# A hybrid decoder layer on one core: the residual written out in two halves, an accumulator fetched in five parts, and the last token tile in block order

## The chip, the core and the metric

The kernel runs on one core of one Trainium2 chip. The metric is the time of one execution on the device in microseconds (us). Three timed runs of the kernel before gave 2352.08, 2352.68 and 2355.79 us; their median, 2352.68 us, is the time before. One more execution was recorded with a profile.

The engines are named as the profile names them: PE is the matrix engine (PEld its weight loads), DVE the vector engine, ACT the scalar engine, POOL the general engine, and SP the engine that issues most of the DMA transfers. A "q" behind the name (SPq) means the sequencer of that engine. SP's transfers run on queue 1 (hardware_dynamic) and POOL's on queue 0 (software_dynamic) of the same 16 DMA engines.

## The reference

One layer over 512 tokens, with 16 learned meta tokens ahead of them (528 rows), model width 2048, feed-forward width 5632, all in float32. The first half of the layer is a mixer of two groups of heads (a gated short convolution and a linear recurrence with decay) and an output projection. What the change touches comes after it:

```python
mix = jnp.concatenate([y_conv, y_rwkv], axis=-1) @ w_out
h = h + rmsnorm(mix, g_post_mix)                       # the residual
f = conv_glu(rmsnorm(h, g_pre_ffn), w_gate_up, conv_ffn, w_down)
h = h + rmsnorm(f, g_post_ffn)
return h[:, N_META:]

def conv_glu(x, w_gate_up, conv_ffn, w_down):
    gu = x @ w_gate_up
    gate, up = jnp.split(gu, 2, axis=-1)
    gate = causal_dwconv(gate, conv_ffn)               # three taps along the tokens
    return (jax.nn.silu(gate) * up) @ w_down
```

The residual h is thus needed twice: normalized, as the input of the feed-forward part, and at the very end, when the normalized result of that part is added to it.

## The kernel before, in words

**Data.** In the first half the activations lie transposed: the model dimension on 128 partitions in 16 tiles h(0) to h(15), the tokens along the free dimension. Matmuls are done in a reduced float32 form, each operand split into a high and a low part ("hi", "lo"; H and O for weights), and the product taken as three matmuls.

**The feed-forward part** has 5632 = 44 tiles of 128 features (f = 0 to 43), in 11 groups of four. A step `seven(f)` makes gate and up of one f in seven products of half matrices, after a Strassen scheme; each product is a *unit* of the main loop. When a group's four f are done, its products with `w_down` are added to an accumulator: `down7` with 14 units for groups 1 to 9, `down` with eight units for the first group (four blocks of 512 columns by two parts), and `last_part` for the last group. The first units that concern the change are units 7 to 14 of the main loop, those of the first down group.

**The accumulator.** Its rows of tokens 256 to 511 stay on the chip in the tile `acc`. Those of tokens 0 to 255 are added in DRAM (`accd`), and so is one of the Strassen products that is kept aside (`acce`). Near the end `reload` brings both back: accd in three fetches on SP into the tiles `hb` and `hs`, and acce in two transfers on POOL that add onto `acc`, all at one place, three units behind the first unit of f = 41.

**One memory, two lives.** The tiles that later are `hb`, `hs` and `acc` first hold the residual: h(0) to h(5) in hb, h(6) and h(7) in hs, h(8) to h(15) in acc. The residual must be out of them before the new contents come: acc is first written behind unit 8, hs in the last part of f = 4's own chain (unit 10) and hb in that of f = 6.

**Turning the residual** (`turned`): the residual must be written to `out` with tokens as rows, so that the tail can fetch it again. In 16 steps (four m-tiles by 128 tokens each) DVE turns four blocks with STREAM_TRANSPOSE into a buffer, hxh and hxl in turn, and SP writes the buffer out in four transfers. These two buffers are also used, afterwards, for the high and low part of hidden activations. The steps are taken in the loops of f = 2 and f = 3, and what is left is run after them.

**The order of work.** A class `Plan` records operations and lays them out by rank (a lower rank goes first) and estimated cost; `plan.step(3)` gives its operations rank 3, the ordinary rank is 2, and matmuls that may fill gaps have the rank `FILL` (9). The mixer, f = 0 to 3 and the tail are laid out so. In the main loop the order of PE, DVE, ACT and POOL is that of the code, unit after unit: the matmuls of unit k, what follows unit k-1, the events of unit k, and the preparation of unit k+2. `at(k, fn)` adds an event to unit k. The order of SP in the main loop isn't the code's: a scheduler sets it. Each engine works through its instructions in order.

**The tail** (`last_part`, `finish`): the token tiles are done as (2, 3), then 0, then 1. For each tile and each block n of 512 columns, twelve matmuls (four f by three products) end a sum in PSUM, DVE adds it to the accumulator, ACT squares and sums the row, and the block is multiplied by the norm's weights gp. When all four blocks are in, the row's scale is computed by small operations (`rb`), and `finish` scales the row, adds the residual, fetched from `out` into a tile of the name tt, and writes the result.

Of the kernel before, what the change touches and what calls it, by code (L numbers as in the profile page):

```python
# [10 lines left out]
F32 = mybir.dt.float32  # L11
F32R = mybir.dt.float32r
AF = mybir.ActivationFunctionType
ALU = mybir.AluOpType
# [73 lines left out]

HEAD3 = 4.0

# [421 lines left out]
def hymba(tc, I, out, ysp=None):  # L512
# [59 lines left out]
    def run(g):  # L572
        for _ in g:
            pass
# [684 lines left out]
    with ExitStack() as ctx2:  # L1259
# [377 lines left out]

        def turned():


            for m in range(0, KT, 4):
                for i in range(0, SEQ, 128):
                    t = p2.tile([128, 2 * HW], F32, name=("hxh", "hxl")[i // 128 % 2], bufs=1)[:, :512]
                    v = t.rearrange("p (j m c) -> p j m c", j=4, m=4)
                    for k in range(4):
                        V.transpose(v[:, :, k], h(m + k)[:, 2 + i:130 + i].rearrange("p (j c) -> p j c", j=4))
                    for q in range(4):
                        c = 512 * q + 32 * m
                        SP.dma_start(out[i:i + 128, c:c + 128].rearrange("(j b) c -> b j c", j=4),
                                     t[32 * q:32 * q + 32].rearrange("p (j c) -> p j c", j=4))  # L1650
                    yield
# [53 lines left out]
        su = sums(T2, T3)  # L1705
        tr = turned()
# [24 lines left out]
        run(su)  # L1731
        with plan.step(3):
            run(tr)

# [45 lines left out]
        def seven(f):  # L1780
# [62 lines left out]
            if f < NF - 1:  # L1843
# [135 lines left out]

        def reload():  # L1980
            acc01.extend([p2.tile([128, 3072], F32, name="hb", bufs=1), p2.tile([128, 2, 512], F32, name="hs", bufs=1)])
            SP.dma_start(acc01[0][:, :2048], accd[1])
            SP.dma_start(acc01[0][:, 2048:], accd[0, :, :1024])
            SP.dma_start(acc01[1].rearrange("p n c -> p (n c)"), accd[0, :, 1024:])
            for t in range(2):
# [71 lines left out]
        m2 = st[:, :4]  # L2057
        r3 = {}

        def last_part(i):  # L2060
# [4 lines left out]

            def down_some(t, n, o, ii):
                for f in ii:
                    with plan.step(2, FILL):
                        down_pe(NG - 1, t, o, lambda f: last_w(2 * n + f // 2), (f,))

            early = {(n, t): bank(t) for n in range(0 if i else 2) for t in ts}
            for n, t in early:
                down_some(t, n, early[n, t], range(GF - 1))
            for n in range(D // 512):
                for t in ts:
                    o = early.get((n, t)) or bank(n if len(ts) == 1 else t)
                    down_some(t, n, o, range(GF - 1 if (n, t) in early else 0, GF))
                    with plan.step(0 if n == 3 else 2):
                        add_up(NG - 1, t, n, o)
                        if i == 0 and n == 1 and t == ts[0]:  # L2080
# [3 lines left out]
                        x = total(t, n)  # L2084
                        S.activation(out=junk[:, 2 * n + t % 2], in_=x, func=AF.Square,
                                     accum_out=st[:, 4 + 4 * t + n:5 + 4 * t + n])
                    with plan.step(3):
                        (G if i == 0 and n < 3 else V).tensor_tensor(out=x, in0=x, in1=gp[:, 512 * n:512 * n + 512], op=ALU.mult)
            for t in ts:
                a = st[:, 20 + 8 * t:28 + 8 * t]  # L2090
                ss, m, r, q, o = (a[:, k:k + 1] for k in range(5))
                with plan.step(0):
                    V.tensor_reduce(out=ss, in_=st[:, 4 + 4 * t:8 + 4 * t], axis=AX.X, op=ALU.add)
                    V.scalar_tensor_tensor(out=m, in0=ss, scalar=1.0 / D, in1=m2[:, t:t + 1], op0=ALU.mult, op1=ALU.add)
                    rsqrt_guess(m, r, q)
                    S.activation(out=r, in_=r, func=AF.Copy, scale=-0.5)
                    V.scalar_tensor_tensor(out=o, in0=q, scalar=-3.0, in1=r, op0=ALU.add, op1=ALU.mult)
                r3[t] = o

        def finish(t):  # L2100
            to = out[128 * t:128 * t + 128]
            if t != LAST[-1][0]:
# [3 lines left out]
                return  # L2106
            x = total(t, 3)
            S.activation(out=x, in_=x, func=AF.Copy, scale=r3[t])
            G.tensor_tensor(out=x, in0=x, in1=hh[:, 1536:], op=ALU.add)
            for n in range(3):  # L2110
                x = total(t, n)
                V.scalar_tensor_tensor(out=x, in0=x, scalar=r3[t], in1=hh[:, 512 * n:512 * n + 512], op0=ALU.mult,
                                       op1=ALU.add)
                SP.dma_start(to[:, 512 * n:512 * n + 512], x)
            SP.dma_start(to[:, 1536:], total(t, 3))

# [98 lines left out]
```

## Time and profile before

| what | value |
|---|---|
| median of the three timed runs | 2352.68 us (2352.08 to 2355.79) |
| the profiled execution | 2357.65 us |
| its span, first to last instruction | 2355.7 us |
| its mean granted PE clock | 0.993 of full speed |
| PE busy | 2307.1 us, 98% of the span |
| DVE, ACT, POOL busy | 1847.3, 1357.1, 661.4 us |
| bytes moved by DMA | 347.58 MB, mean 148 GB/s |

A row of a timeline or of the chain of waits begins with the start in us from the span's first instruction, then the length in us, then engine, source line, operation, out<-in by the program's names, shapes and "xN" for N instructions in one row; brackets at the end tell how long the engine stood idle before and what released it. All instructions of the recorded parts have the line of the recording helper, L231, so they are told apart by tile. Rows of a window give its length and the busy time and number of instructions of PE, PEld, DVE, ACT and POOL, then the granted PE clock, the busy share of the DMA engines and GB/s.

### The profile page before, as it was taken

How to read it: one execution, taken by the hardware profiler on the slowest of the kernel's cores; microseconds unless marked ns; L12 is line 12 of the kernel's file. 1: busy time of each engine (PE TensorE's matmuls, PEld its weight loads, DVE VectorE, ACT ScalarE, POOL GpSimd, SP SyncE). 2: the span in 40 equal slices, each digit the busy share in tenths (PEclk: the TensorE clock that was granted, in tenths of full speed). 3: DMA queues.
4: the chain of work that ended last, by engine and by line, in shares of the span. 5: the costliest groups of instructions: out<-in, count | busy, mean ns of one | idle time of the engine just before them, and what ended most of it. 6: DMA issues, size and time to landing. Idle time of an engine off the chain costs nothing.

```text
span 2355.7 us, 46510 instructions
## 1 busy us (share of the span) xinstructions
PE 2307.1 (98%) x18032; PEld 2180.4 (93%) x18032; DVE 1847.3 (78%) x2612; ACT 1357.1 (58%) x2653; POOL 661.4 (28%) x887
## 2 busy tenths in 40 slices
PE   9999999999999999997999999999999999999998
PEld 8999999999999999996998989898989898989896
DVE  7687898878754677785598879797978888888776
ACT  7666766767654556663455555555555555555545
POOL 0131746455351012510012131313131313131312
PEclk9999999999999999998999999999999999999999
DMA  5544333333433755745448494858584848585765
GB/s 183 156 132 118 88 96 89 103 103 107 127 105 90 226 174 162 157 112 131 124 121 210 126 215 126 207 133 206 131 208 118 212 128 200 131 193 139 189 182 139
DMA packets 169954, 347.58 MB, mean 148 GB/s; under 512 B 35682, under 2 KB 56548, under 8 KB 169092
## 3 DMA queue, kind: packets, MB, share of 16 engines
q1 hardware_dynamic: 135492, 269.07, 36.7%
q0 software_dynamic: 34240, 75.53, 19.3%
q8 instruction: 142, 2.33, 0.4%
q14 instruction: 80, 0.66, 0.1%
HBM read 279.11 MB, written 65.42 MB: 146 GB/s over the span
## 4 chain that ended last, share of the span: by engine, by line
PE 85%; DVE 5%; DMA 4%; issue 2%; ACT 2%; POOL 1%; SPq 1%; DVEq 0%; ACTq 0%; POOLq 0%
PE mps L231 56%; PE u L231 14%; PE d L231 8%; PE st L231 4%; PE aux L231 2%; DVE O L231 2%; ACT H L231 1%; DVE raw L231 1%; SPq L231 1%; DMA R<-w_gu_dram 1%; DMA R<-w_down_dram 0%; DVE acc L231 0%; DMA l<-lo 0%; DMA hs<-xT_dram 0%; DMA hb<-xT_dram 0%
## 5 line engine op out<-in xcount | busy, mean ns | idle before, releaser
L231 DVE TENSOR_TENSOR O<-R,H 128x1024 fp32r<-128x1024 f32 x455 | 598.3, 1315 | 171.4 <-ACT H L231 152.4
L231 ACT CAST H<-R 128x1024 fp32r<-128x1024 f32 x455 | 470.2, 1049 | 158.8 <-PE u L231 60.4
L231 PE MATMUL mps<-ahi,whi 128*128 128x264 f32 (+2 forms) x1792 | 359.9, 289 | 6.1 <-ACT ahi L231 5.6
L231 PE MATMUL mps<-alo,whi 128*128 128x264 f32 (+2 forms) x1792 | 360.5, 289 | 0.3 <-DVE alo L231 0.2
L231 PE MATMUL mps<-ahi,wlo 128*128 128x264 f32 (+2 forms) x1792 | 358.4, 288 | 1.2 <-DVE wlo L231 1.0
L231 POOL TENSOR_TENSOR raw<-raw,rb 128x514 f32<-128x514 f32 (+2 forms) x45 | 93.6, 2080 | 736.7 <-DVE raw L231 503.7
L231 PE MATMUL mps<-tt,H 128*128 128x258 f32 (+1 forms) x2160 | 288.6, 284 | 5.3 <-ACT H L231 4.5
L231 PEld LDWEIGHTS mps<-ahi,whi 128*128 128x128 f32 x1792 | 273.8, 189 | 8.9 <-ACT ahi L231 5.6
L231 DVE TENSOR_TENSOR wlo<-raw,whi 128x512 fp32r<-128x512 f32 (+1 forms) x261 | 193.8, 748 | 109.8 <-ACT whi L231 90.6
L231 PEld LDWEIGHTS mps<-tt,H 128*128 128x128 f32 x2160 | 273.3, 190 | 6.8 <-ACT H L231 4.7
L231 PEld LDWEIGHTS mps<-ahi,wlo 128*128 128x128 f32 x1792 | 273.8, 189 | 3.8 <-DVE wlo L231 1.6
L231 PE MATMUL mps<-ahi,H 128*128 128x258 f32 (+1 forms) x1064 | 259.3, 284 | 18.4 <-DVE raw L231 16.4
L231 PEld LDWEIGHTS mps<-alo,whi 128*128 128x128 f32 x1792 | 273.8, 189 | 3.4 <-DVE alo L231 1.2
L231 PE MATMUL mps<-alo,H 128*128 128x258 f32 (+1 forms) x1064 | 259.3, 283 | 0.5 <-DVE alo L231 0.5
L231 ACT CAST whi<-raw 128x512 fp32r<-128x512 f32 (+1 forms) x261 | 156.7, 604 | 162.9 <-PE mps L231 87.3
L231 DVE TENSOR_TENSOR R<-R 128x1024 f32<-128x1024 f32 x190 | 232.6, 1224 | 5.2 <-DMA R<-w_down_dram 1.4
L231 PEld LDWEIGHTS mps<-ahi,H 128*128 128x128 f32 x1064 | 199.8, 191 | 19.0 <-ACT H L231 16.5
L231 PEld LDWEIGHTS mps<-alo,H 128*128 128x128 f32 x1064 | 199.7, 191 | 0.7 <-DVE alo L231 0.7
L231 POOL TENSOR_SCALAR SUV<-VT 32x64 f32<-32x64 f32 x272 | 129.2, 475 | 161.4 <-PE st L231 136.9
L231 PE MATMUL mps<-ahi,O 128*128 128x258 f32 (+1 forms) x1064 | 158.2, 284 | 0.0
L231 PE MATMUL mps<-tt,O 128*128 128x258 f32 (+1 forms) x1080 | 153.6, 282 | 0.0
L231 PEld LDWEIGHTS mps<-ahi,O 128*128 128x128 f32 x1064 | 141.4, 191 | 0.0
(396 smaller groups left out, 4490.3 us busy)
## 6 DMA issues: line engine op xcount, KB each, us to landing
R<-w_gu_dram SPq DMA_DIRECT2D x176, 512.0 KB, 5.6
raw<-w_in_dram SPq DMA_DIRECT2D x208, 256.0 KB, 2.7
R<-w_down_dram SPq DMA_DIRECT2D x88, 512.0 KB, 4.6
R<-w_gu_dram POOLq DMA_DIRECT2D x40, 512.0 KB, 6.2
accd<-raw POOLq DMA_DIRECT2D x54, 256.0 KB, 6.6
accd<-q POOLq DMA_DIRECT2D x54, 256.0 KB, 7.4
R<-w_down_dram POOLq DMA_DIRECT2D x18, 512.0 KB, 7.8
raw<-w_out_dram SPq DMA_DIRECT2D x32, 256.0 KB, 3.9
```

Source lines behind the costliest of these rows:

```text
L231: return getattr(self.real, op)(*real, **{k: x.get() if isinstance(x, View) else x for k, x in kw.items()})
```

## The change

It has three parts.

1. `turned` becomes one step with the buffer as its argument. The eight steps of the acc half (m = 8 and 12) are taken in the loop of f = 3, at the ordinary rank. The eight steps of the half in hb and hs (m = 4, then 0) become `aside(i)`, two per unit in units 10 to 13, into buffers of the names raw and q. The last part of f = 4's chain, which overwrites hs, moves three units later.
2. `reload` gets an argument, and its five transfers are placed 8, 10, 12, 14 and 16 units behind the first unit of f = 41.
3. In `last_part` the twelve matmuls of a block of tiles 0 and 1 become one step with a rank of its own, so that blocks come in order; the sum of the first three columns of squares is taken and scaled with block 2, the row's scale takes one ACT step less on the way (gp is scaled by -0.5 beforehand), and the multiplies by gp are POOL's for tiles 2 and 3, all eight, and DVE's for the others. `finish` of the last tile has three multiply-adds of 768, 768 and 512 columns on DVE with one transfer each, in place of three of 512 on DVE with a fourth block on ACT and POOL.

```diff
-HEAD3 = 4.0
+HEAD3, ENDS = 4.0, ((0, 768), (768, 1536), (1536, 2048))
...
-        def turned():
-            for m in range(0, KT, 4):
+        def turned(t, m, i):
+            v = t.rearrange("p (j m c) -> p j m c", j=4, m=4)
+            for k in range(4):
+                V.transpose(v[:, :, k], h(m + k)[:, 2 + i:130 + i].rearrange("p (j c) -> p j c", j=4))
+            for q in range(4):
+                c = 512 * q + 32 * m
+                SP.dma_start(out[i:i + 128, c:c + 128].rearrange("(j b) c -> b j c", j=4),
+                             t[32 * q:32 * q + 32].rearrange("p (j c) -> p j c", j=4))
+
+        def turns():
+            for m in (8, 12):
                 for i in range(0, SEQ, 128):
-                    t = p2.tile([128, 2 * HW], F32, name=("hxh", "hxl")[i // 128 % 2], bufs=1)[:, :512]
...
+                    turned(p2.tile([128, 2 * HW], F32, name=("hxh", "hxl")[i // 128 % 2], bufs=1)[:, :512], m, i)
                     yield
...
-                            with plan.step(3):
-                                next(tr, None)
+                        if f == 3:
+                            next(tr, None)
...
-        with plan.step(3):
-            run(tr)
+        run(tr)
...
-                    at(e - 1 + (i if i < n - 1 or f % GF else 9 if g == 1 else 11 if n == 6 else 16), step, i)
+                    at(e - 1 + (i + 3 * (i > 3 and f == GF) if i < n - 1 or f % GF else 9 if g == 1 else 11 if n == 6 else 16), step, i)
...
+        def aside(i):
+            turned(two().rearrange("p a b -> p (a b)")[:, :512] if i % 2 else wide()[:, :512], 0 if i > 3 else 4, 128 * (i % 4))
+
+        for i in range(8):
+            at(10 + i // 2, aside, i)
...
-                    at(len(units) + 3, reload)
+                    for i, k in enumerate((8, 10, 12, 14, 16)):
+                        at(len(units) + k, reload, i)
...
-            def down_some(t, n, o, ii):
-                for f in ii:
-                    with plan.step(2, FILL):
+            def down_some(t, n, o, ii, rank):
+                with plan.step(2, rank):
+                    for f in ii:
                         down_pe(NG - 1, t, o, lambda f: last_w(2 * n + f // 2), (f,))
...
+                    if i:
+                        turn[0] += 1
+                        down_some(t, n, o, range(GF), FILL + turn[0] / 100)
...
+                        if n == 2:
+                            V.tensor_reduce(out=s, in_=a[:, :3], axis=AX.X, op=ALU.add)
+                            V.scalar_tensor_tensor(out=s, in0=s, scalar=1.0 / D, in1=m2[:, t:t + 1], op0=ALU.mult,
+                                                   op1=ALU.add)
+                        if n == 3:
+                            V.scalar_tensor_tensor(out=m, in0=a[:, 3:], scalar=1.0 / D, in1=s, op0=ALU.mult, op1=ALU.add)
+                            S.activation(out=r, in_=m, func=AF.Abs_reciprocal_sqrt)
+                            V.scalar_tensor_tensor(out=q, in0=m, scalar=r, in1=r, op0=ALU.mult, op1=ALU.mult)
+                            V.scalar_tensor_tensor(out=r, in0=q, scalar=-3.0, in1=r, op0=ALU.add, op1=ALU.mult)
+                            r3[t] = r
+                    with plan.step(3 if i < 2 else 2):
+                        (V if i else G).tensor_tensor(out=x, in0=x, in1=gp[:, 512 * n:512 * n + 512], op=ALU.mult)
...
+            for a, b in ENDS:
+                x = acc01[0][:, a:b]
+                V.scalar_tensor_tensor(out=x, in0=x, scalar=r3[t], in1=hh[:, a:b], op0=ALU.mult, op1=ALU.add)
+                SP.dma_start(to[:, a:b], x)
...
+        S.activation(out=gp, in_=gp, func=AF.Copy, scale=-0.5)
```

How the instructions move is seen in the order in which they stand on each engine. On DVE, between the end of f = 3 and the first steps of f = 4, before (the number behind a name is that of the buffer; acc is the residual's second half, O<-R,H the low part of a weight tile, mps the sums of PE in PSUM):

```order
L231 STREAM_TRANSPOSE hxh_15018<-acc_12790 128x4x32
L231 STREAM_TRANSPOSE hxl_15185<-acc_12790 128x4x32 x4
L231 TENSOR_TENSOR raw_15281<-mps_15081,q_15180 128x258
L231 STREAM_TRANSPOSE hxh_15198<-acc_12790 128x4x32 x4
L231 STREAM_TRANSPOSE hxl_15204<-acc_12790 128x4x32 x4
L231 STREAM_TRANSPOSE hxh_15216<-acc_12790 128x4x32 x4
L231 STREAM_TRANSPOSE hxl_15222<-acc_12790 128x4x32 x4
L231 STREAM_TRANSPOSE hxh_15234<-acc_12790 128x4x32 x4
L231 STREAM_TRANSPOSE hxl_15240<-acc_12790 128x4x32 x4
L231 TENSOR_TENSOR hxl_15287<-raw_15034,hxh_15285 128x512
L231 TENSOR_TENSOR O_15291<-R_14728,H_15289 128x1024
L231 TENSOR_TENSOR raw_15318<-mps_14983,q_15138 128x256
```

The step that reads mps and ends this piece stands behind six steps of four transposes. The same place in the changed kernel:

```order
L231 TENSOR_TENSOR O_15178<-R_14871,H_15171 128x1024
L231 TENSOR_TENSOR raw_15209<-mps_15074,q_15175 128x258
L231 TENSOR_TENSOR hxl_15215<-raw_15042,hxh_15213 128x512
L231 TENSOR_TENSOR O_15219<-R_14658,H_15217 128x1024
L231 TENSOR_TENSOR raw_15246<-mps_15012,q_15107 128x256
```

No transpose is left here. Those of acc now stand further ahead, among the rows of f = 3 (the first is row 1155 of DVE, the last row 1234, and this place begins at row 1290), and those of hb and hs stand in units 10 to 13, where before only the rows of O stood. The beginning of that place on DVE, in the changed kernel:

```order
L231 TENSOR_TENSOR O_15401<-R_15280,H_15399 128x1024
L231 STREAM_TRANSPOSE raw_15427<-hb_11636 128x4x32 x2
L231 STREAM_TRANSPOSE raw_15427<-hs_12517 128x4x32 x2
L231 STREAM_TRANSPOSE q_15436<-hb_11636 128x4x32 x2
L231 STREAM_TRANSPOSE q_15436<-hs_12517 128x4x32 x2
L231 TENSOR_TENSOR O_15448<-R_15317,H_15446 128x1024
L231 STREAM_TRANSPOSE raw_15486<-hb_11636 128x4x32 x2
```

On SP, the transfers of the same units in the changed kernel:

```order
L231 DMA R_15504<-w_gu_dram 128x1024
L231 DMA out_dram<-raw_15427 32x4x128 x4
L231 DMA out_dram<-q_15436 32x4x128 x4
L231 DMA accd_15387<-raw_15478 128x512
L231 DMA accd_15387<-q_15481 128x512
L231 DMA out_dram<-raw_15486 32x4x128 x4
L231 DMA out_dram<-q_15495 32x4x128 x4
L231 DMA R_15552<-w_gu_dram 128x1024
L231 DMA R_15614<-w_gu_dram 128x1024
L231 DMA out_dram<-raw_15534 32x4x128 x4
```

In every unit eight writes to out stand among the writes of the accumulator (accd) and the loads of weights (R), where before those two were alone.

At the reload, POOL before (acc<-acce is the transfer that adds; raw<-raw,rb the scaling of hidden activations):

```order
L231 DMA R_27222<-w_gu_dram 128x1024
L231 DMA acc_15464<-acce_16741 128x2x512 x2
L231 TENSOR_TENSOR raw_27358<-raw_27358,rb_14284 128x514
L231 DMA R_27459<-w_gu_dram 128x1024
L231 TENSOR_TENSOR raw_27592<-raw_27592,rb_14284 128x514
```

And POOL in the changed kernel:

```order
L231 DMA R_27222<-w_gu_dram 128x1024
L231 TENSOR_TENSOR raw_27351<-raw_27351,rb_14271 128x514
L231 DMA R_27452<-w_gu_dram 128x1024
L231 TENSOR_TENSOR raw_27588<-raw_27588,rb_14271 128x514
L231 DMA acc_15392<-acce_16741 128x2x512 x2
```

The two transfers move behind a weight load and two scalings. On SP the three fetches of accd stand, before and after, between the same two loads of w_gu: five loads ahead of them, then hb, hs, hb, then seven loads.

More of the change, by code (lines that the diff above doesn't have):

```diff
@@ L1705, in hymba @@
         su = sums(T2, T3)
-        tr = turned()
+        tr = turns()
         for f in (2, 3):
@@ L1978, in hymba, with reload @@
         acc01 = []
[L1980 to L1985, printed above, removed]
+        def reload(i):
+            if i == 0:
+                acc01.extend([p2.tile([128, 3072], F32, name="hb", bufs=1), p2.tile([128, 2, 512], F32, name="hs", bufs=1)])
+                SP.dma_start(acc01[0][:, :2048], accd[1])
+            elif i == 1:
+                SP.dma_start(acc01[0][:, 2048:], accd[0, :, :1024])
+            elif i == 2:
+                SP.dma_start(acc01[1].rearrange("p n c -> p (n c)"), accd[0, :, 1024:])
+            else:
+                t = i - 3
                 G.dma_start(acc[:, t].rearrange("p (e h c) -> p e h c", e=2, h=2)[:, :, 1],
                             acce[t].rearrange("p (e c) -> p e c", e=2), accum_op=ALU.add)
+        def aside(i):
+            turned(two().rearrange("p a b -> p (a b)")[:, :512] if i % 2 else wide()[:, :512], 0 if i > 3 else 4, 128 * (i % 4))
+        for i in range(8):
+            at(10 + i // 2, aside, i)
         for f in range(4, NF):
@@ L2058, in hymba @@
         r3 = {}
+        turn = [0]
         def last_part(i):
@@ L2084, in last_part @@
                         x = total(t, n)
[L2085 to L2098, printed above, removed]
+                        S.activation(out=junk[:, 2 * n + t % 2], in_=x, func=AF.Square, accum_out=a[:, n:n + 1])
+                        if n == 2:
[10 more added lines that the diff above has]
+                        (V if i else G).tensor_tensor(out=x, in0=x, in1=gp[:, 512 * n:512 * n + 512], op=ALU.mult)
         def finish(t):
```

27 lines of the change are left out of this document (8 added, 19 removed).

## The prediction

> **What bounds the kernel now.** I read the page first, then the waits of PE (the TensorE matmuls), then stretches of 20 us around each long wait, then the chain that ended last.
>
> ```profile
> span 2355.7 us, 46510 instructions
> PE 2307.1 (98%) x18032; PEld 2180.4 (93%) x18032; DVE 1847.3 (78%) x2612; ACT 1357.1 (58%) x2653; POOL 661.4 (28%) x887
> ```
>
> PE is busy for 2307.1 of 2355.7 us, and the change takes no matmul away. So it can gain only where PE stands, where PE runs at a lower clock, and behind the last matmul. The waits of PE (engine and tile, releaser, total us, times, longest):
>
> ```profile
> PE mps L231 <- DVE raw L231: 16.4, 1, 16.4
> PE mps L231 <- ACT ahi L231: 7.6, 2, 5.6
> PE mps L231 <- ACT H L231: 4.5, 1, 4.5
> PE d L231 <- DVE acc L231: 2.8, 9, 0.3
> ```
>
> Two of these lie where the change works. The columns of the windows are window, length, busy PE, PEld, DVE, ACT, POOL, granted clock, DMA share, GB/s:
>
> ```profile
> 1060.00:1080.00 20.00, 20.00 (x170) 20.00 (x169) 15.10 (x29) 7.68 (x14) 1.61 (x1) 1.00 0.42 114
> 1080.00:1100.00 20.00, 3.65 (x23) 3.47 (x22) 10.06 (x30) 3.46 (x4) 0.86 (x1) 0.64 0.50 107
> ...
> 1120.00:1140.00 20.00, 20.00 (x88) 16.07 (x87) 5.46 (x5) 8.57 (x12) 0.09 (x1) 1.00 0.47 143
> ...
> 2240.00:2260.00 20.00, 15.48 (x121) 15.07 (x120) 8.07 (x10) 5.85 (x8) 1.80 (x3) 0.91 1.00 286
> 2280.00:2300.00 20.00, 20.00 (x170) 20.00 (x170) 16.80 (x21) 11.13 (x17) 2.38 (x3) 1.00 0.36 106
> ```
>
> PE is full at 1060, nearly empty at 1080, full again at 1120; at 2240 it misses 4.5 us while the DMA engines are at 1.00. After both holes the clock is low, and the chain shows its price beside the same work at full speed:
>
> ```profile
> 1097.66 5.37 PE mps L231 x24
> ...
> 1162.11 2.83 PE u L231 x24
> ...
> 2111.80 14.34 PE mps L231 x120
> ...
> 2257.86 17.04 PE mps L231 x120
> ```
>
> 24 matmuls took 5.37 us after the first hole and 2.83 at full speed (2.5 lost); 120 took 17.04 after the second and 14.34 at full speed (2.7 lost). At stake are 16.4 + 2.5 = 18.9 us and 4.5 + 2.7 = 7.2 us.
>
> By the Trainium skill, "TensorE: Matmul & The Clock Gate", Part 1, an idle PE falls to half clock and needs about 3.4 us of activity to come back; half speed for 3.4 us would be an estimated loss of 1.7 us a hole, and the whole gain 1.8 us smaller. The trace loses 2.5 and 2.7, and that decides.
>
> **Part 1, the residual turned in two halves.** DVE around the first hole:
>
> ```profile
> 1080.76 0.89 DVE L231 STREAM_TRANSPOSE hxh<-acc 128x128 f32<-128x128 f32 x4 [4.58 <-DMA out_dram<-hxh]
> ...
> 1095.35 0.69 DVE L231 TENSOR_TENSOR hxl<-raw,hxh 128x512 fp32r<-128x512 f32 x1 [3.25 <-DMA out_dram<-hxl]
> ...
> 1097.09 0.42 DVE L231 TENSOR_TENSOR raw<-mps,q 128x256 f32<-128x256 f32 x1
> ```
>
> Each step of four transposes fills hxh or hxl and must wait until that buffer's last contents have landed in out. The read of mps at 1097.09, which frees the PSUM bank that PE needs, stands behind these steps in DVE's in-order queue. Nothing is slow there; PE waits for a copy of the residual that nobody needs before the tail. In the changed order the transposes of acc stand between row 1155 and row 1234 of DVE, and none remains ahead of that read. hxh and hxl are then free much earlier, so the cast behind them, which waited too, doesn't take its place. I take the full **18.9 us**; bounds 0 (the wait changes its name) and 18.9.
>
> What it adds: the other eight steps run two per unit in units 10 to 13, about 1120 to 1142. They bring 8 x 0.89 = 7.1 us of DVE and 32 DMA issues on SP:
>
> ```profile
> 1092.12 1.76 SPq L231 DMA_DIRECT2D out_dram<-hxl  x4
> DMA to landing us min/median/max: 1.6/1.8/4.7
> ...
> 1110.10 0.59 ACT L231 COPY raw<-d 128x512 f32<-128x512 f32 x1 [0.34 <-PE d L231]
> 1121.28 0.59 ACT L231 COPY raw<-d 128x512 f32<-128x512 f32 x1 [0.35 <-PE d L231]
> 1156.73 1.05 ACT L231 CAST H<-R 128x1024 fp32r<-128x1024 f32 x1
> ```
>
> That is 8 x 1.76 = 14.1 us of SP. Two away copies two units apart start 11.2 us after each other, so a unit takes 5.6 us and the four 22.4. DVE is busy 5.46 of 20 us there and gets 7.1 more, which is less than the 15.10 it carries at 1060 with PE full; a cast of O waits behind at most two steps, 1.8 us. On SP, weight loads stand behind each eight DMAs, and the new buffers (raw and q) are those of the away copies of the accumulator, so a later copy on ACT waits for a landing. A pair of steps takes 2 x 0.89 + 2 x 1.76 + 1.8 = 7.1 us end to end if nothing overlaps, against a unit of 5.6: a drift of at most 4 x 1.5 = 6 us. The first weight loads behind such writes, in unit 11 at about 1134, are those whose casts begin at 1156.73 before, so more than 15 us are there for the landing and the drift. I price it at **0**, since this hides it; uncovered, it is the 6 us.
>
> **The planned order in front** is also redone (ranks changed), since the transposes of the acc half now compete at normal rank with the work of f = 3. Nothing in the trace prices this. The nearest rows are the small waits of PE, 2.8 us over nine places and less in the rest. Bounds: a gain of 1 and a loss of 3; I take a loss of **1**.
>
> **Part 2, the accumulator fetched in five parts.** At the second hole:
>
> ```profile
> 2238.11 2.14 POOL L231 DMA_DIRECT2D acc<-acce  x1
> ...
> 2244.22 28.48 SPq L231 DMA_DIRECT2D R<-w_gu_dram  x7
> 2244.22 12.44 DMA R<-w_gu_dram
> 2256.76 1.99 ACT L231 CAST H<-R 128x1024 fp32r<-128x1024 f32 x2 [10.67 <-DMA R<-w_gu_dram]
> 2252.26 1.10 PE L231 MATMUL mps<-ahi,O 128*128 128x256 f32 x8
> 2257.86 3.81 PE L231 MATMUL mps<-tt,H 128*128 128x258 f32 x16 [4.50 <-ACT H L231]
> ```
>
> PE waits for the cast of a weight load that took 12.44 us. It was issued only after the accd fetches on SP, and it shared the DMA engines with the two acce accumulates of 512 KB on POOL's queue. The diff spreads all five DMAs, yet in the program only POOL's pair moves: SP's three fetches of accd stand ahead of the same w_gu load as before. The accumulates move behind two further POOL issues of weights and their scalings, about 40 us later, near the window at 2280 with a DMA share of 0.36; there nothing waits for them.
>
> How much of the load's delay is theirs? In the two parts of the load's time before and after 2250 and in the 2 us ahead of it (queue, packets, MB, share of 16 engines):
>
> ```profile
> q0 software_dynamic: 180, 0.40, 107.8%
> ...
> q0 software_dynamic: 274, 0.53, 72.1%
> q1 hardware_dynamic: 137, 0.56, 36.7%
> ...
> q1 hardware_dynamic: 632, 2.80, 86.4%
> q0 software_dynamic: 136, 0.24, 16.5%
> ```
>
> These are 2244 to 2246, 2246 to 2250, and 2250 to 2258. Queue 0 used 0.72 x 4 + 0.165 x 6.66 = 4.0 us of the engines' time between 2246 and the landing at 2256.66, and up to 1.9 us before. Without it the load lands 4.0 to 5.9 us earlier, at 2250.8 to 2252.7. Landing to first matmul took 2257.86 - 2256.66 = 1.2 us, so PE could start at 2252.0 to 2253.9; its work before ends at 2252.26 + 1.10 = 2253.36. What stays is a wait of 0 to 0.5 us, too short to show a low clock here. Gain **7.0 us** of 7.2; the other end is 0, if the loads are held by what SP itself issued ahead.
>
> By the Trainium skill, "DMA: Bandwidth & Descriptors", section Queues, rings and completion order, an engine alternates between queues packet by packet, so the loads would get about half while the accumulates last; by this rule they end at the same 4.0 us earlier. The trace has 72 against 37 % there.
>
> **Part 3, the tail.** Behind the last matmul:
>
> ```profile
> 2345.06 0.40 PE L231 MATMUL d<-ahi,hxl 128*128 128x512 f32 x1
> 2345.49 0.69 DVE L231 TENSOR_TENSOR hb<-hb,d 128x512 f32<-128x512 f32 x1
> ...
> 2347.30 0.15 DVE L231 TENSOR_REDUCE rb<-rb 128x1 f32<-128x4 f32 x1
> ...
> 2348.61 3.08 DVE L231 SCALAR_TENSOR_TENSOR hb<-hb,rb,tt 128x512 f32<-128x512 f32 x3
> 2349.39 2.66 SPq L231 DMA_DIRECT2D out_dram<-hb  x4
> ...
> 1106.18 1.53 DVE L231 SCALAR_TENSOR_TENSOR raw<-raw,par 128x512 f32<-128x512 f32 x2
> ```
>
> The chain of small steps from the last square to the large multiply-adds starts these 2348.61 - 2345.49 = 3.1 us after the last addition. The change takes one scalar step on DVE and two on ACT out of it (the three columns before are summed and scaled ahead of time); at 0.15 us for a step, as the sum of the four columns takes, that is 0.45, and I take 0.4 out: 2348.2. The three multiply-adds of 512 columns ran beside POOL at 3.08 / 3 = 1.03 us each; elsewhere two took 1.53. Now all 2048 columns are DVE's: 4 x 0.77 = 3.1 us, or 4.1 at the slower pace. So the last DMA is issued at 2351.3 or 2352.3, against 2352.05 - 0.66 = 2351.4 (the last of four). Bounds: 0.9 later, and 0.7 earlier if the chain loses 1.0; the slower pace is that beside POOL, which has nothing to do there now, so I take a gain of **0.2**. The twelve matmuls of a block in order make the last blocks close one after another rather than together, so DVE's additions of earlier blocks are done when the last block ends; PE's work is the same; the scaling of gp by ACT (128x2048) and POOL's two further multiplies lie beside matmuls.
>
> **Sum.** 18.9 + 7.0 + 0.2 - 1 = 25.1 us; I take 25. The profiled run took 2357.65 us (span 2355.7 and 1.95 outside it), so it would be 2332.4; it is itself 5.0 us above the median of 2352.68. From the median the forecast is 2352.7 - 25 = **2328 us**.
>
> **The rivals.**
>
> *The second hole stays.* SP's order is unchanged at the fetch, and the load was issued at 2244.22 behind 2 MB of accd. If that holds it and the accumulates only filled gaps, PE still waits. For it: queue 1 runs at 86 % after 2250, so the engines are nearly full without queue 0. Against: 72 % of the engines for queue 0 in the four us when the load began. Gain 18.9 + 0.2 - 1 = 18.1: 2334.6 us.
>
> *A new wait of a few us.* The two steps per unit or the new plan hold up a weight load or a PSUM read: the 6 us above plus a low clock of 2.5, or the 3 of the plan. For it: SP carries 14.1 us of issues in 22, ahead of weights. Against: the landing of 1.8 us and DVE's free time. 25 less 4 to 10: 2332 to 2338 us.
>
> *Slower: the output writes chain in units 10 to 13.* Eight steps with two buffers, their landings queued with the weight loads; the DMA share was 0.47 there before, and loads of that size have taken 12.44 us where it was 1.00. If a landing takes L, the four pairs take 4 x (0.9 + 3.5 + L) if nothing overlaps, and with 12.4 us for L that is 67 us against the 22.4 of the units; minus the 15 us of cover, PE stands 30 us, and the time is 2328 + 30 = 2358. It decides from where the loss passes 25 us: L of 11 us. The longest landing above is 4.7, with eight transfers of that kind in a row.
>
> **How the numbers follow.** The forecast has 0.58, the second hole 0.22, the new wait 0.15 and the slower case 0.05. The likeliest case by itself spans 2324 to 2331 (the plan's gain of 1 to loss of 3, the tail by 0.9 either way, and some 2 us for the spread of runs, 2352.08 to 2355.79 before). The range of 8 in 10 takes in the second hole: 2323 to 2338. About 0.2 %, 4.7 us, is what a measurement of this kernel can tell from no change. Faster by more than that takes the first three cases but for a corner of the third: 0.93; within it 0.03; slower 0.04.
>
> **What would show it.** Right: no wait of PE for raw near 1080 and the granted clock at 1.00 in the 20 us after; transposes from hb into raw and q in units 10 to 13 with PE at 20.00 of 20 us; acc<-acce some 40 us later and the w_gu load behind accd in 7 us rather than 12.44; the last output issue within 6 us of the last matmul. Wrong: a wait of PE for ACT H near the accd fetch at its old size (the second hole stays), a wait for H, O or a raw copy in the first down group (the new wait or the slower case), or transposes of acc that still wait for landings and hold the read of mps.

## The result

Four runs of the changed kernel have a median of 2327.96 us (2326.37 to 2334.25), four of the kernel before 2353.41 us (2352.08 to 2355.79): a ratio of 0.9896 with a 95% interval of 0.9876 to 0.9916. That is 25.5 us, or 1.04%, faster; the forecast was 2328 us and 25 us. The profiled execution took 2334.25 us, the slowest of its four, with a span of 2332.4 us, against 2357.65 and 2355.7 before: 23.3 us less in the span.

The page of the changed kernel:

```profile
span 2332.4 us, 46500 instructions
PE 2303.0 (99%) x18032; PEld 2174.3 (93%) x18032; DVE 1848.4 (79%) x2614; ACT 1356.8 (58%) x2645; POOL 661.7 (28%) x888
```

PE has the same 18032 matmuls and is busy 4.1 us less for them. The waits of PE that stood at 16.4 (for raw) and 4.5 us (for H) before:

```profile
PE mps L231 <- ACT ahi L231: 6.2, 2, 5.5
PE d L231 <- DVE acc L231: 2.8, 9, 0.3
...
PE mps L231 <- ACT q L231: 1.9, 2, 1.0
...
PE mps L231 <- ACT H L231: 0.5, 1, 0.5
```

No wait for raw is left in mps, and the one for H is 0.5 us. The windows (columns as before):

```profile
1080.00:1100.00 20.00, 20.00 (x99) 16.61 (x98) 8.77 (x16) 7.28 (x11) 3.02 (x2) 1.00 0.66 184
1100.00:1120.00 20.00, 20.00 (x87) 16.13 (x86) 10.20 (x29) 8.73 (x13) 0.48 (x1) 1.00 0.82 235
...
2220.00:2240.00 20.00, 18.49 (x153) 18.08 (x152) 10.86 (x12) 7.79 (x11) 2.31 (x3) 1.00 0.95 268
```

The first down group now lies at 1080 to 1127; the 32 added transposes and writes show in DVE (10.20) and in the DMA share (0.82), and PE is full at full clock. At the fetch near 2230, 1.5 us of PE are still missing, at full clock. Where the two profiles part is read from landmarks that both chains of waits hold (x120 is a row of 120 matmuls). First before, then after:

```profile
1005.67 10.46 PE mps L231 x87
1147.76 14.34 PE mps L231 x120
...
2111.80 14.34 PE mps L231 x120
...
2277.73 17.20 PE mps L231 x144
```

```profile
1004.18 10.46 PE mps L231 x87
...
1127.39 14.34 PE mps L231 x120
...
2093.87 14.34 PE mps L231 x120
...
2255.44 17.20 PE mps L231 x144
```

| stretch | before | after | less by |
|---|---|---|---|
| start to the last steps of the mixer (x87) | 1005.67 | 1004.18 | 1.5 |
| to the first full group (first x120): **part 1** | 142.09 | 123.21 | 18.9 |
| eight full groups | 964.04 | 966.48 | -2.4 |
| around the fetch (x144): **part 2** | 165.93 | 161.57 | 4.4 |
| to the end of the last matmul | 67.73 | 67.69 | 0.0 |
| last matmul's end to the end: **part 3** | 10.24 | 9.27 | 1.0 |

The first and the third row are in parts of the program where the change does nothing to speak of. Over the profiles of the runs below, the first landmark lies between 1003.0 and 1005.7 where the start of the program is left alone, and the eight groups last 962.8 to 965.6 us; the changed kernel's own second profile has 963.71. So both rows are what one execution differs from another, and the 966.48 of this one is at the long end.

### The profile page after: what moved, and what is told of

It is laid out like the page before. It is cut to its first block, busy times and chain, and to the rows that moved or that the text cites. A ratio compares the mean times of both kernels' runs of the same rounds, so it can differ in the third digit from the quotient of the medians.

```text
span 2332.4 us, 46500 instructions
## 1 busy us (share of the span) xinstructions
PE 2303.0 (99%) x18032; PEld 2174.3 (93%) x18032; DVE 1848.4 (79%) x2614; ACT 1356.8 (58%) x2645; POOL 661.7 (28%) x888
## 4 chain that ended last, share of the span: by engine, by line
PE 88%; DVE 5%; DMA 3%; issue 2%; ACT 2%; POOL 1%; SPq 0%; DVEq 0%; ACTq 0%; POOLq 0%
PE mps L231 58%; PE u L231 15%; PE d L231 8%; PE st L231 4%; PE aux L231 3%; DVE O L231 2%; DMA R<-w_gu_dram 1%; DMA hs<-xT_dram 1%; DVE raw L231 1%; ACT H L231 0%; DVE acc L231 0%; DMA l<-lo 0%; DMA accd<-q 0%; ACT q L231 0%; DMA accd<-raw 0%
## 5 line engine op out<-in xcount | busy, mean ns | idle before, releaser
L231 ACT COPY q<-mps 128x258 f32<-128x258 f32 x132 | 49.6, 376 | 157.0 <-PE mps L231 126.1
```

The lines of the kernel that those rows point to most:

```text
L231: return getattr(self.real, op)(*real, **{k: x.get() if isinstance(x, View) else x for k, x in kw.items()})
```

## The experiments

The stretches of the table serve as measures, since they leave out what varies elsewhere. "Stretch 1" is that of part 1, "stretch 2" that of part 2, "tail" the last row.

### Each part alone

**Part 1 alone**: the diff of the change with `reload`, `last_part` and `finish` as before.

> The kernel before with part 1 alone (residual turned in two halves). Theory (the landing waits of the transposes in front of the read of mps cost 16.4 us of PE and 2.5 us of clock): no wait of PE for raw, 18.9 us less than before, with 1 us for the new order of the plan 17 to 20 us less; the second hole (wait for ACT H, 4.5 us) stays. Rival (the new order of the plan, not the wait, makes the gain, or the wait comes back under another name): less than 15 us.

Measured: 2337.21 us (2334.97 to 2338.70) against 2355.42 us, ratio 0.9921 (0.9907 to 0.9934), 18.2 us less. Stretch 1 is 123.21 us, as in the changed kernel and 18.9 less than before. Stretch 2 is 165.96 us, as before (165.93). Waits of PE:

```profile
PE mps L231 <- ACT ahi L231: 5.7, 1, 5.7
PE mps L231 <- ACT H L231: 4.7, 1, 4.7
PE d L231 <- DVE acc L231: 2.8, 9, 0.3
```

The wait for raw is gone, and that for H stays. Nothing of the 18.9 us came back.

**Part 2 alone**:

```diff
-        def reload():
+        def reload(i):
...
-                    at(len(units) + 3, reload)
+                    for i, k in enumerate((8, 10, 12, 14, 16)):
+                        at(len(units) + k, reload, i)
```

> The kernel before with part 2 alone; in the program only the two acce accumulates on POOL move, behind one weight load and two scalings. Theory (queue 0 took 4.0 us of the DMA engines' time from the w_gu load): the load issued behind accd takes 8.4 us instead of 12.4, the wait for ACT H shrinks from 4.5 to 0.5 us and the clock stays full, 5 to 7 us less than before. Rival (the accd fetches ahead of the load on SP hold it): no change, within 1 us.

Measured: 2348.53 us (2344.57 to 2351.13), ratio 0.9971 (0.9961 to 0.9982), 6.9 us less. In this program PE, DVE, ACT and SP have the same order as before; POOL's two accumulates alone stand elsewhere. Stretch 2 is 158.30 us, 7.6 less than before, and in it only two waits of 0.3 us remain. The rival of the same order on SP falls: the fetches of accd stay ahead of the loads, and the hole goes. The load behind them lands after 7.1 us, not 12.4.

**Part 3 alone**: `last_part`, `finish` and the scaling of gp.

> The kernel before with part 3 alone (last token tile's blocks in order). Theory: last matmul to the end of the span 9.3 us instead of 10.2, nothing else moves, 0.2 to 1.0 us less than before, too little for the total to tell from no change. Rival (the new ranks of the matmuls in the tail open waits of PE there, or PE starts the tail later): as long as before or longer.

Measured: 2354.13 us (2350.54 to 2357.72), ratio 0.9991 (0.9982 to 1.0), 1.3 us less and within what can't be told from no change. The tail is 9.59 us. With the tail as before, five profiles show 10.24, 9.75, 10.24, 10.16 and 9.54 us (mean 9.99); with the new one, eight show 8.84 to 9.59 us (mean 9.20): 0.8 us less. The parts add up: 18.2 + 6.9 + 1.3 = 26.4 us, against 25.5 for all three.

### What made the first hole

**Transposes without writes**: the kernel before, its 32 writes of the acc half left out.

```diff
-                    for q in range(4):
+                    for q in range(4 if m < 8 else 0):
...
+        def fill(i):
+            SP.dma_start(out[128 * i:128 * i + 128].rearrange("p (q c) -> p q c", q=4)[:, :, 256:],
+                         I["w_down"][1, i].rearrange("p (q c) -> p q c", q=4))
```

> The kernel before, with the transposes of the acc half kept but their 32 writes to out left out (four plain transfers of weights fill these columns later, so the output lacks that half). Theory (the hole is made of waits for landings, the transposes themselves are 0.9 us a step): the wait of PE for raw falls from 16.4 us to 5 us at most, 11 to 19 us less than before. Rival (DVE's work itself, sixteen more transposes ahead of the read, makes the hole): the wait stays above 10 us.

Measured: 2348.78 us, ratio 0.9972 (0.9962 to 0.9982). The total can't be used: the four transfers that fill the columns depend on nothing, and were issued at 12.5 to 20.9 us of the span instead of later, so PE is some 7 us late already in the mixer (the chain's x166 of mps starts at 748.95 instead of 741.36), well ahead of stretch 1. Stretch 1 is 128.56 us, 13.5 less than before. DVE and PE in it:

```profile
1083.20 2.73 DVE L231 STREAM_TRANSPOSE hxh<-acc 128x128 f32<-128x128 f32 x12
1085.86 3.62 DVE L231 STREAM_TRANSPOSE hxl<-acc 128x128 f32<-128x128 f32 x16
1089.59 0.69 DVE L231 TENSOR_TENSOR hxl<-raw,hxh 128x512 fp32r<-128x512 f32 x1
...
1091.33 0.42 DVE L231 TENSOR_TENSOR raw<-mps,q 128x256 f32<-128x256 f32 x1
```

```profile
1091.90 0.36 PE L231 MATMUL mps<-ahi,H 128*128 128x256 f32 x1 [3.48 <-DVE raw L231]
...
1091.90 4.52 PE mps L231 x24
```

28 transposes still stand ahead of the read, back to back in 6.3 us, and PE waits 3.5 us instead of 16.4. So 13 of the 16.4 us were waits for landings; the rest is the transposes' own time. The profile of before agrees. Between the two rows of the prediction stand

```profile
1084.88 0.89 DVE L231 STREAM_TRANSPOSE hxh<-acc 128x128 f32<-128x128 f32 x4 [2.40 <-DMA out_dram<-hxh]
1086.86 0.89 DVE L231 STREAM_TRANSPOSE hxl<-acc 128x128 f32<-128x128 f32 x4 [1.08 <-DMA out_dram<-hxl]
1089.00 0.89 DVE L231 STREAM_TRANSPOSE hxh<-acc 128x128 f32<-128x128 f32 x4 [1.26 <-DMA out_dram<-hxh]
1091.01 1.09 DVE L231 STREAM_TRANSPOSE hxl<-acc 128x128 f32<-128x128 f32 x4 [1.11 <-DMA out_dram<-hxl]
```

and with the 4.58 and 3.25 us shown there, DVE's six waits for landings add up to 13.7 us. In the run without the writes the clock loses 4.52 - 2.83 = 1.7 us here. 3.5 + 1.7 = 5.2 of the 5.35 us by which the stretch is longer than 123.21.

**The acc half at rank 3 again**:

```diff
                         if f == 3:
-                            next(tr, None)
+                            with plan.step(3):
+                                next(tr, None)
...
-        run(tr)
+        with plan.step(3):
+            run(tr)
```

> The changed kernel with the acc half's transposes put back to rank 3 (behind other work), as all of them were before; only the halving of their number stays. If the halving makes the gain, eight steps find their gaps ahead of the read of mps even so, and the stretch takes 123.2 us as in the changed kernel. If the rank makes it, transposes come late and PE waits for raw again, some us of the 16.4.

Measured: 2330.63 us (2329.11 to 2332.14) against 2354.12 us, ratio 0.9898 (0.9883 to 0.9912). Stretch 1 is 123.20 us. In this program the last transpose of acc stands at DVE's row 1271 instead of 1234, and the read of mps at 1294. In the profiles that last transpose starts at 1058.9 us instead of 1033.0, and the read at 1077.0 in both, so the transposes come later but still ahead of the trouble. Halving their number (the eight steps stay in the loop of f = 3) makes the gain; the rank adds nothing.

### What the moved half costs

**Without the eight steps in units 10 to 13** (the two lines of `at(10 + i // 2, aside, i)` out, a `fill` for the other columns in).

> The changed kernel without the eight steps in units 10 to 13: neither the transposes of the hb and hs half nor their 32 writes; in their place four plain transfers of weights fill these columns of out about a hundred units later, so the output lacks half of the residual. Theory (DVE and SP have room in units 10 to 13, the addition costs nothing): the time of the changed kernel within 0.5 us in that stretch. Rival (the writes delay the weight loads or the away copies): up to 6 us less.

Measured: 2335.61 us, ratio 0.9920 (0.9904 to 0.9937), so in total slower than the changed kernel. Again the filling transfers are at the start of the program (12.6 to 20.4 us) and the chain's x166 starts at 748.17. Stretch 1 is 123.22 us, with the steps 123.21: their cost is 0.0 us.

**Four steps per unit**, in units 10 and 11, and then **all eight in unit 10**:

```diff
-            at(10 + i // 2, aside, i)
+            at(10 + i // 4, aside, i)
```

> The changed kernel with the eight aside steps four per unit, in units 10 and 11, instead of two per unit in units 10 to 13. By my sum two pairs of steps take 14.2 us in a unit of 5.6 if nothing overlaps, a drift of 17 us against a cover of 15: about 2 us of waiting for a weight cast or an away copy, at most 5. Rival (steps overlap through three buffers of each name): no wait, the changed kernel's time. Slower than by 10 us would say that the slow case of the prediction was close.

Measured: 2329.58 us (2327.57 to 2331.12), ratio 0.9893 (0.9879 to 0.9908); stretch 1 is 123.22 us. No wait, so the 2 us of my sum were too many and the rival of overlapping steps held: SP issued the four steps of unit 10 one behind the other, from 1096.99 to 1104.66 us, 1.9 us a step.

> The changed kernel with all eight aside steps in unit 10. Four steps per unit cost nothing in the first down group, so the sum of the prediction (a pair of steps takes 7.1 us end to end, 15 us of cover) is too dark somewhere. By that sum four pairs in one unit last 28 us against 5.6, a drift of 23 us against 15 of cover: 8 us of PE waiting in the first down group. If the pairs overlap through the three buffers of each name, issuing on SP alone counts, 14 us in all, which the cover of 15 holds: the stretch from the last steps of the mixer to the first full group stays at 123.2 us.

Measured: 2337.07 us (2335.69 to 2338.59) against 2354.12 us, ratio 0.9925 (0.9910 to 0.9940). Stretch 1 is 130.67 us, 7.5 longer. Its waits of PE, and the rows of ACT and of the chain:

```profile
PE d L231 <- ACT raw L231: 4.8, 1, 4.8
```

```profile
1109.71 0.59 ACT L231 COPY raw<-d 128x512 f32<-128x512 f32 x1 [8.62 <-DMA out_dram<-raw]
...
1118.69 1.05 ACT L231 CAST H<-R 128x1024 fp32r<-128x1024 f32 x1 [5.98 <-PE u L231]
```

```profile
1107.86 1.76 DMA out_dram<-raw
...
1110.35 5.44 PE d L231 x12
1115.79 2.80 PE u L231 x12
```

The away copy of the accumulator (raw<-d, the read that frees PE's bank) waits for a raw buffer whose write to out hasn't landed; PE stands 4.8 us, and the low clock costs 5.44 - 2.80 = 2.6. The eight us of my sum came nearly out, but by luck, since the steps overlap and no weight cast was late. What gives first in these units is the three buffers of the name raw, not the weights loaded ahead. A landing takes 1.8 us in the median here, 3.2 at most, and the chain from 1095 to 1130 us shows that landings are only a third of what keeps the buffer:

```profile
DMA to landing us min/median/max: 1.7/1.8/3.2
```

```profile
by line: PE d L231 34.2%; PE u L231 24.0%; SPq L231 10.5%; DMA out_dram<-raw 10.3%; DVE raw L231 6.7%; issue 5.6%; DVE q L231 4.4%; ACT H L231 2.7%; ACT raw L231 1.7%; DVEq L231 0.3%; ACTq L231 0.1%; DVE O L231 0.1%
```

SP's issues hold 10.5%, the landings 10.3% and the transposes into raw and q 11.1%. SP issues the 32 writes without a pause, from 1098.54 to 1114.15 us, and the write that the copy waits for stands behind 16 others.

### What made the second hole

**The other half: accd late, acce at its old place**. A memset of one column by DVE ahead of each fetch makes SP issue them behind four, five and eight further weight loads.

```diff
+                V.memset(acc01[0][:, :1], 0.0)
+                SP.dma_start(acc01[0][:, :2048], accd[1])
...
-                    at(len(units) + 3, reload)
+                    for i, k in enumerate((8, 10, 12, 3, 3)):
```

> The kernel before, with the accd fetches on SP held back (a one-column memset of the target by DVE at units 8, 10 and 12) and the two acce accumulates on POOL left where they were: the other half of what part 2 says. If 2 MB of accd ahead of the w_gu load are as much to blame as the accumulates, the wait for ACT H goes and 5 to 7 us are gained, so either of the two alone would do. If the accumulates alone are to blame, the wait stays near 4.5 us and nothing is gained.

Measured: 2348.17 us (2345.20 to 2353.13) against 2355.37 us, ratio 0.9972 (0.9962 to 0.9981), 7.2 us less. Stretch 2 is 158.59 us; in it PE waits 0.8 and 0.7 us for copies and not for H. So either half of part 2 is enough, in the same size. The accumulates by themselves are not to blame; the load was late because 2 MB of accd stood ahead of it in SP's queue and the accumulates shared the engines at the same time. That is seen in this one load in all profiles, those of the next experiment included:

| beside the load or just ahead of it | profiles | from issue to landing, us |
|---|---|---|
| accd and the accumulates | before, parts 1 and 3 alone, transposes without writes | 12.4 to 12.8 |
| accd, not the accumulates | changed (two), part 2 alone, rank 3, without the eight steps, four and eight per unit | 7.0 to 8.4 |
| the accumulates, not accd | accd late | 8.2 |
| neither | both late, both late with uneven pieces | 5.7, 5.8 |

With accd late the load is also issued 2 to 3 us earlier than before, counted from the start of stretch 2.

**Both halves**, in the changed kernel, and the same again with the last pieces 896, 768 and 384 columns wide, beside the changed kernel itself:

> The changed kernel, with the three accd fetches held back too: a one-column memset of the target by DVE at units 8, 10 and 12 stands ahead of each, so SP issues them behind five to eight further weight loads. Theory (what is left of the second hole, 0.5 us, and two waits of about 1 us near it come from the crowd of DMAs around the fetch): the load takes under 7 us, those waits go, 1 to 3 us less than the changed kernel, 26 to 28 less than before. Rival (accd late collides with the w_down loads of the tail): PE waits for a weight cast near the last units, as long as the changed kernel or longer.

> The changed kernel once more, to stand beside the next one on the same chip: about 2328 us, 1.0 to 1.2 per cent less than before. The stretch around the second hole, 161.6 us in its profile against 158.3 where no wait is left, shows whether those 3.3 us are its own (161 to 162 again) or vary by execution (anything down to 158.3).

> The changed kernel with the accd fetches held back by memsets, and the last tile finished in pieces of 896, 768 and 384 columns instead of 768, 768 and 512. Theory: the stretch around the second hole at 158.3 us, up to 3 us less than the changed kernel in the same job; the last multiply-add and its transfer are a quarter shorter, 0.2 us of the tail. Rival (the rest of the hole comes and goes in the changed kernel too): within 1 us of it, not to be told apart.

| kernel | us, median and extremes | ratio to before | stretch 2 | tail |
|---|---|---|---|---|
| both late | 2327.76 (2326.47 to 2329.94) | 0.9884 (0.9870 to 0.9897) | 158.27 | 9.21 |
| changed, again | 2329.81 (2327.21 to 2332.34) | 0.9894 (0.9879 to 0.9909) | 160.10 | 9.27 |
| both late, uneven pieces | 2328.82 (2327.87 to 2329.22) | 0.9889 (0.9872 to 0.9905) | 159.34 | 9.44 |

The second and the third stood beside each other on one chip. In the changed kernel, and in others with part 2, stretch 2 varies from one execution to the next: 161.57 and 160.10 in the changed kernel itself; 159.51 without the eight steps, 160.10 and 158.36 with four and eight per unit, 159.94 with rank 3, and 158.30 in part 2 alone. The crowd around the fetch still costs 0 to 3 us. With both halves late it was 158.27 and 159.34. That may be 1 or 2 us better, but the intervals of the totals cover each other, so whether it beats the changed kernel stays open. The uneven pieces bring nothing that the tail shows.

## Why the prediction was right, and where it wasn't

**The forecast** of 2328 us met 2327.96, and the forecast of 25 us less met 25.5, or 24.3 in the second comparison of the same kernel (2354.12 against 2329.81). The mechanism was right in its two large terms. That the time is met to 0.04 us is luck: the four runs of the changed kernel spread over 7.9 us, and the terms erred both ways. The plan in front cost nothing that shows instead of 1 us, the tail gave 0.8 instead of 0.2, and part 2 gave 4.4 and 5.8 us in the two profiles of the changed kernel instead of 7.0.

**Part 1** was worth what the trace said: 16.4 + 2.5 = 18.9 us forecast, 18.88 in the stretch, 18.2 in the total. The chain of causes (landing, transposes, read of mps in DVE's queue, PE) is shown by the writes' removal: it took 13 of the 16.4 us, and the remaining 3.5 is transposes. The forecast of nothing for the added work is shown too, by its removal.

**The cover in units 10 to 13 was named wrongly.** The prediction had over 15 us of weights loaded ahead as the cover, and a drift of up to 6 us if pairs of steps don't overlap. The runs show that pairs do overlap, that four steps per unit still cost nothing, and that the first thing to give, with eight, is the buffer of the away copy. The prediction saw that copy's wait as one of two dangers and gave it no number.

**The order in front.** No run shows the charge of 1 us for the new plan: stretch 1 contains the plan's last part and is shorter by the full 18.9; ahead of it the difference is within the 2.7 us by which executions vary, so a cost of 1 us there can't be excluded.

**Part 2.** The size was right: 7.0 forecast; 7.6 in stretch 2 and 6.9 in the total where it was made alone. In the changed kernel's own profile the load's chain is

```profile
2219.32 8.03 DMA accd<-q
...
2227.84 8.42 DMA R<-w_gu_dram
```

8.42 us instead of 12.44: the 4.0 us that the sum had taken out for queue 0, with the 0.5 us of waiting for H that the sum left at most. (The 7 us named at the end of the prediction, as what would show it, did not follow from its own sum, which gives 8.4.) That profile gains only 4.4 us in the stretch, since two other waits of 1.0 us show in it:

```profile
PE mps L231 <- ACT q L231: 1.0, 1, 1.0
PE u L231 <- ACT raw L231: 1.0, 1, 1.0
```

and since executions differ by up to 3 us there. The cause as the prediction put it, the accumulates, holds for this change, but it is half the story: the rival that blamed accd ahead on SP was wrong that the hole would stay, and right that accd alone could be blamed as well.

**Part 3** was mis-sized: 0.2 us forecast and 0.7 at most, 0.8 between the means of five and of eight tails. Two terms of its sum were off. The first is the multiply-adds:

```profile
2325.38 0.41 DVE L231 SCALAR_TENSOR_TENSOR rb<-rb 128x1 f32<-128x1 f32 x2
2325.82 2.61 DVE L231 SCALAR_TENSOR_TENSOR hb<-hb,rb,tt 128x768 f32<-128x768 f32 x3
...
2326.87 1.92 SPq L231 DMA_DIRECT2D out_dram<-hb  x3
```

2048 columns took 2.61 us, not 3.1, less than 1536 took before (3.08). They start 2325.82 - 2323.17 = 2.65 us after the last addition's start, 0.5 earlier than before (3.12), where 0.4 was forecast. The issues end 2326.87 + 1.92 - 2323.13 = 5.7 us after the last matmul, before 2352.05 - 2345.46 = 6.6. The second, worth 0.3 us, is the end before, with which the sum compared:

```profile
L231 SPq DMA_DIRECT2D out_dram<-hb x4: 332/338/346, 2349.4 to 2351.7; - x4
```

An issue lasts 0.33 us, so the last of the four began at 2351.7; the prediction had taken a quarter of the whole row, 0.66 us, and 2351.4.

**The rivals.** "The second hole stays" fell with part 2 alone. The "new wait of a few us" appeared only in small, as the 1.0 us waits. The slower case would have needed eight steps in one unit and more: even then the kernel gains 0.75%, and the landing stayed at 1.8 us. In units 10 to 13 of the changed kernel it is 2.6 us in the median and 4.9 at most, far from the 11 us that the slower case needed.

## What to carry to other kernels

A wait of PE that starts with a transfer's landing is best removed by asking which instruction in the in-order queue it holds up: the copy that nobody needed soon stood ahead of the read that PE needed, and moving half of it behind unrelated work cost nothing. What a stall costs is the wait plus the slow matmuls after it, both read from the trace. When several transfers crowd one moment, moving either group away may give the whole gain, so the second move can be worth nothing; and room in a busy stretch can be bounded by the buffer that the added work borrows, so ask what the buffer waits for: here the transposes, the queue's issues and the landing in about equal parts.

## What was not expected of the hardware

The price of the low clock after a wait varied with little relation to the wait's length: 1.7 us after 3.5 us (transposes without writes), 2.7 after 4.5, 2.6 after 4.8 and 2.5 after 16.4; after the wait of 1.0 us in the changed kernel the clock stayed at 1.00. By the Trainium skill, "TensorE: Matmul & The Clock Gate", Part 1, some 3.4 us at half clock give an estimated 1.7 us; the first of these agrees with it and the others are larger. Waits for H of 4.4 us (part 3 alone), 4.7 (part 1 alone) and 4.8 (transposes without writes) cost 1.8, 2.8 and 1.8 us. The windows of the low clock show what the price follows: before, its two holes; then transposes without writes; then eight steps in unit 10.

```profile
2256.50:2263.33 6.83, 5.47 (x25) 5.47 (x26) 5.46 (x5) 3.88 (x5) 2.97 (x2) 0.50 0.37 143
1085.73:1102.80 17.07, 5.14 (x24) 5.17 (x25) 7.59 (x19) 3.46 (x4) 2.11 (x1) 0.50 0.58 141
...
1093.09:1096.50 3.41, 3.41 (x18) 3.41 (x17) 1.26 (x2) 0.05 (x1) 2.13 (x1) 0.50 0.91 309
...
1108.78:1115.61 6.83, 5.26 (x12) 4.12 (x13) 1.23 (x1) 2.99 (x5) 0.00 (x0) 0.50 0.59 150
```

The granted clock was 0.50 for 3.41, 6.83 or 17.07 us: once, twice or five times 3.41. Half of the time in which PE works in such a window is lost: 5.47, 5.14, 3.41 and 5.26 us of work give 2.7, 2.6, 1.7 and 2.6 us, which are the prices above. In the third window the clock falls only 1.2 us after PE has started again at 1091.90. So the price is set by how much of these windows lies behind the wait, and waits of nearly the same length can cost 1.8 or 2.8 us.

DVE's last multiply-adds took 2.61 us for 2048 columns (1.27 ns a column) in the changed kernel and 3.08 us for 1536 (2.0 ns) in the kernel before. The rows by length (min, median and max in ns) show that the width isn't the reason; the first two are of before, the last of the changed kernel:

```profile
L231 DVE SCALAR_TENSOR_TENSOR hb<-hb,rb,tt x3: 746/752/1750, 2348.6 to 2349.9; 128x512 f32<-128x512 f32 x3
2349.42 1.73 POOL L231 TENSOR_TENSOR hb<-hb,tt 128x512 f32<-128x512 f32 x1 [8.49 <-ACT hb L231]
...
L231 DVE SCALAR_TENSOR_TENSOR hb<-hb,rb,tt x3: 746/1012/1020, 2325.8 to 2327.7; 128x768 f32<-128x768 f32 x2, 128x512 f32<-128x512 f32 x1
```

Before, two of the three took 0.75 us each, as the one of 512 columns does in the changed kernel, and the third, begun at 2349.95 beside POOL's addition, took 1.75. So the 1.03 us each of the prediction was the mean of unequal times. In all five profiles with the tail of before the longest is 1.75 us; in the eight with the new one, where POOL has no addition there, none of 512 columns takes more than 0.75. That the addition holds the third is likely but not shown by itself: the second overlaps its first 0.6 us and isn't longer.
